# A matrix product with seven-product blocks: a third row pair multiplied directly before the summed pairs begin

## The chip, the cores and the metric

The kernel runs on one core of a Trainium2 chip. The metric is the device time of one execution in microseconds (us). A profile of one execution per run gives a span, from the first to the last recorded instruction, which is shorter than the time. TensorE multiplies, VectorE and ScalarE empty its accumulators (PSUM) and convert types, GpSimd converts and adds, SyncE issues most transfers. The trace also holds the clock that TensorE was granted, as a share of full speed; 0.50 is called cold. A record is one entry of the trace, with a start and a length.

## The reference

```
x: 16 x 512 x 768 fp32        w_qkv: 768 x 2304 fp32
qkv = matmul(x, w_qkv)
return stack([qkv[..., :768], qkv[..., 768:1536], qkv[..., 1536:]])
```

It is one product of an 8192 x 768 matrix with a 768 x 2304 matrix, cut into three parts.

## The kernel before

Rows are taken in 32 pairs of 128-row blocks. The 2304 columns are two quads of 1024 and a remainder of 256. A quad of a pair takes seven block products of three matmuls, 21 in place of 24, if sums of rows and of weights are formed first. These sums are not there at the start, so the first two pairs are multiplied directly in bf16, one weight block of 512 columns after the other, while the rest of the weights comes in. Pair 2 is the first summed one: TensorE turns its fp32 rows so that GpSimd can sum them.

```
def block(q, c, w, groups, cast_next):        # direct, for pairs 0 and 1
    ps = [bank() for _ in range(4)]
    for js, tiles in groups:
        for n in tiles:                       # 4 row blocks
            ... matmul(ps[n], xb[p][:, j, rows], w[:, j, :]) for j in js
            ... cast_next(p); copy ps[n] to the output tile; store
...
busy(11)                                      # warming matmuls on zeros
cast_rows(0); turn_bf16(0)
busy(4)
cast_rows(1); ...; turn_bf16(1)
...
cast(0, 1, 1, bt0, nc.gpsimd)                 # second half of the next block
nc.gpsimd.tensor_copy(out=b22[0][:], in_=stage[0, 1, 1])
block(0, 0, b1[0], singles, lambda h: None)   # 24 matmuls
rem(0)                                        # 12 matmuls of 256 columns
rem(1)
turn_fp32(2)                                  # TensorE turns fp32 rows
cast(0, 0, 1, bt0, act)                       # first half of the next block
round_x(2)
sums_x(2)
...
block(0, 1, bt0, halves, cast_next(1, 0, b1[1]))
block(1, 0, b1[1], halves, cast_next(1, 1, bt1))
block(1, 1, bt1, halves, lambda h: None)
...
for p in range(2, NP): two(quad(p, 0), quad(p, 1), early)   # summed pairs
```

## Time and profile before

| | before |
|---|---|
| time, median of 3 (lowest to highest) | 368.38 us (368.31 to 368.80) |
| the profiled execution: time, span | 369.94, 368.2 us |
| TensorE busy | 98% of the span |
| first summed product starts at | 37.73 us |
| one summed pair | 9.54 + 1.33 = 10.87 us |

The page gives busy shares; the chain that ended last gives, from the first to the last instruction, what held up the end, in pieces of start, length and work. Where the chain is on TensorE without a break, only fewer or faster matmuls help.

### The profile page before, as it was taken

How to read it: one execution, taken by the hardware profiler on the slowest of the kernel's cores; microseconds unless marked ns; L12 is line 12 of the kernel's file. 1: busy time of each engine (PE TensorE's matmuls, PEld its weight loads, DVE VectorE, ACT ScalarE, POOL GpSimd, SP SyncE). 2: the span in 40 equal slices, each digit the busy share in tenths (PEclk: the TensorE clock that was granted, in tenths of full speed). 3: DMA queues.
4: the chain of work that ended last, by engine and by line, in shares of the span. 5: the costliest groups of instructions: out<-in, count | busy, mean ns of one | idle time of the engine just before them, and what ended most of it. 6: DMA issues, size and time to landing. Idle time of an engine off the chain costs nothing.

```text
span 368.2 us, 5286 instructions
## 1 busy us (share of the span) xinstructions
PE 359.8 (98%) x1791; PEld 246.9 (67%) x1791; DVE 229.7 (62%) x235; ACT 185.5 (50%) x307; POOL 191.9 (52%) x191
## 2 busy tenths in 40 slices
PE   7979999999999999999999999999999999999995
PEld 3634666677767677766667776766776666777673
DVE  3399766555666655576655566665557665556632
ACT  4557645454444454544545444445454454544442
POOL 1089935466544456644456654445664444665420
PEclk9989999999999999999999999999999999999998
DMA  7999898889988899998888998888899889899767
GB/s 295 381 385 339 268 281 278 291 280 301 317 283 276 271 302 280 309 310 273 280 292 280 301 316 285 276 278 297 276 313 306 276 261 309 271 309 319 267 232 280
DMA packets 80618, 108.09 MB, mean 294 GB/s; under 512 B 4816, under 2 KB 60368, under 8 KB 80592
## 3 DMA queue, kind: packets, MB, share of 16 engines
q1 hardware_dynamic: 64640, 95.96, 79.8%
q10 hardware_dynamic: 15952, 11.80, 10.1%
q8 instruction: 14, 0.23, 0.3%
q14 instruction: 12, 0.10, 0.1%
HBM read 32.24 MB, written 75.50 MB: 293 GB/s over the span
## 4 chain that ended last, share of the span: by engine, by line
PE 96%; DMA 1%; ACT 1%; DVE 0%; issue 0%
PE ps L212 78%; PE ps L262 12%; PE ps L386 6%; DMA xin<-in_x_dram 1%; PE ps L169 0%; PE ps L158 0%; ACT bt L374 0%; ACT xc L140 0%; ACT xb L140 0%; ACT xf L140 0%; ACT orem L317 0%; DVE xb L139 0%
## 5 line engine op out<-in xcount | busy, mean ns | idle before, releaser
L212 PE MATMUL ps<-t,s 128*128 128x512 f32 x720 | 194.5, 412 | 0.0
L212 PEld LDWEIGHTS ps<-t,s 128*128 128x128 f32 x720 | 133.2, 188 | 32.0
L175 POOL CAST xb<-xf 128x1536 bf16<-128x1536 f32 x30 | 45.5, 1515 | 139.3 <-DVE xf L124 139.3
L212 PE MATMUL ps<-b,xb 128*128 128x512 bf16 x360 | 88.1, 381 | 0.0
L124 DVE STREAM_TRANSPOSE xf<-xin 128x1536 f32<-128x1536 f32 x29 | 86.9, 2996 | 0.9 <-DMA xin<-in_x_dram 0.8
L246 DVE TENSOR_TENSOR o<-o,ps 128x512 f32<-128x512 f32 x60 | 41.3, 688 | 62.4 <-PE ps L212 62.3
L240 DVE TENSOR_TENSOR o<-o,ps 128x512 f32<-128x512 f32 x60 | 41.3, 688 | 57.3 <-ACT o L239 57.3
L212 PEld LDWEIGHTS <-xb 128*128 128x128 bf16 x360 | 30.5, 98 | 44.5 <-issue 15.7
L239 ACT ACTIVATE o<-ps 128x512 f32<-128x512 f32 x60 | 36.0, 600 | 46.8 <-PE ps L212 46.8
L226 ACT ACTIVATE o<-ps 128x512 f32<-128x512 f32 x60 | 35.9, 599 | 45.2 <-DVE o L246 40.6
L233 ACT ACTIVATE o<-ps 128x512 f32<-128x512 f32 x60 | 36.0, 600 | 43.4 <-PE ps L212 43.4
L262 PE MATMUL ps<-w_rem,xb 128*128 128x256 bf16 x384 | 47.5, 273 | 0.0
L212 PE MATMUL ps<-b,s 128*128 128x512 f32 x180 | 46.5, 393 | 0.0
L262 PEld LDWEIGHTS <-xb 128*128 128x128 bf16 x384 | 35.0, 98 | 12.4 <-issue 8.4
L212 PEld LDWEIGHTS ps<-b,s 128*128 128x128 f32 x180 | 33.8, 188 | 8.0
L230 DVE TENSOR_TENSOR o<-o,ps 128x512 f32<-128x512 f32 x60 | 37.6, 669 | 2.0 <-ACT o L226 1.3
L243 ACT ACTIVATE o<-ps 128x512 f32<-128x512 f32 x60 | 35.9, 598 | 4.8 <-ACT orem L317 0.4
L184 POOL TENSOR_TENSOR s<-s,xf 128x384 fp32r<-128x384 f32 x30 | 31.9, 1064 | 2.4
L187 POOL TENSOR_TENSOR s<-xf,s 128x384 fp32r<-128x384 f32 x30 | 32.1, 1069 | 0.0
L183 POOL TENSOR_TENSOR s<-xf 128x384 fp32r<-128x384 f32 x30 | 31.9, 1064 | 0.0
L185 POOL TENSOR_TENSOR s<-xf 128x384 fp32r<-128x384 f32 x30 | 31.6, 1054 | 0.0
L272 ACT ACTIVATE orem<-ps 128x512 f32<-128x512 f32 x31 | 18.6, 599 | 22.7 <-PE ps L262 22.7
(40 smaller groups left out, 122.7 us busy)
## 6 DMA issues: line engine op xcount, KB each, us to landing
out_dram<-o SPq DMA_DIRECT2D x62, 768.0 KB, 4.9
out_dram<-o SPq DMA_DIRECT2D x65, 256.0 KB, 4.6
xin<-in_x_dram SPq DMA_DIRECT2D x60, 192.0 KB, 6.7
xin<-in_x_dram ACTq DMA_DIRECT2D x56, 192.0 KB, 5.7
out_dram<-orem SPq DMA_DIRECT2D x31, 256.0 KB, 2.3
st<-in_w_qkv_dram SPq DMA_DIRECT2D x6, 768.0 KB, 14.1
xin<-in_x_dram SPq DMA_DIRECT2D x3, 768.0 KB, 5.8
st<-in_w_qkv_dram SPq DMA_DIRECT2D x6, 256.0 KB, 6.2
```

Source lines behind the costliest of these rows:

```text
L124: nc.vector.transpose(t[:].rearrange("p j (g b) -> p g j b", b=G), xin.pop(p)[:].rearrange("p g (a j) -> p g j a", a=G),)
L175: nc.gpsimd.tensor_copy(out=xb[p][:], in_=xf[p][:])
L187: g.tensor_tensor(s[:, 4], a12, s[:, 2], op=sub)
L212: nc.tensor.matmul(ps[:], lhs[j], rhs[j], start=(start and j == 0), stop=(j == KH - 1), skip_group_check=True,)
L226: nc.scalar.activation(c11, u.x[:], ident)
L230: nc.vector.tensor_tensor(c11, c11, u.z[:], op=add)
L233: nc.scalar.activation(c12, u.x[:], ident)
L239: nc.scalar.activation(c22, u.x[:], ident)
L240: nc.vector.tensor_tensor(c22, c22, u.y[:], op=add)
L243: nc.scalar.activation(c21, u.x[:], ident)
L246: nc.vector.tensor_tensor(c12, c12, u.y[:], op=add)
L262: nc.tensor.matmul(ps, xb[p][:, j, r * P:(r + 1) * P], w_rem[:, j, :], start=(j == 0), stop=(j == KT - 1), skip_group_check=True,)
```

## The change

It makes three pairs direct instead of two. Pair 2's rows are cast to bf16 by VectorE and turned in bf16, and twelve matmuls of pair 2 on the first weight block stand where TensorE waited for the second block. VectorE casts the second block. Each direct block has six row blocks for four, so the next weights are wanted later. Pair 3 becomes the first summed one.

```
-    cast(0, 1, 1, bt0, nc.gpsimd)
-    nc.gpsimd.tensor_copy(out=b22[0][:], in_=stage[0, 1, 1])
-    block(0, 0, b1[0], singles, lambda h: None)
+    block(0, 0, b1[0], singles, nothing)
     rem(0)
     rem(1)
-    turn_fp32(2)
-    cast(0, 0, 1, bt0, act)
-    round_x(2)
-    sums_x(2)
+    cast_rows(2, False)                      # VectorE alone
+    turn_rows(2, False)                      # bf16, copied out by VectorE alone
+    block(0, 0, b1[0], halves((4, 5)), nothing)
+    for h in range(2):
+        cast(0, h, 1, bt0, dve)
     for n in range(1, 5):
         sum_w(0, n)
-    nc.gpsimd.tensor_copy(out=b22[1][:], in_=stage[1, 1, 1])
-    block(0, 1, bt0, halves, cast_next(1, 0, b1[1]))
+    dve.tensor_copy(out=b22[0][:], in_=stage[0, 1, 1])
+    block(0, 1, bt0, halves(range(6)), cast_next(1, 0, b1[1]))
     ... the other two blocks likewise, then rem(2)
-    for p in range(2, NP):
+    for p in range(3, NP):
```

The fp32 identity matrix and `turn_fp32` go away; the loads of pairs 3 and 4 are issued earlier.

More of the change, by code (lines that the diff above doesn't have):

```diff
@@ L135, in load_rows, with copy_halves, cast_rows @@
         nc.sync.dma_start(xin[p][:], rows.rearrange("(r m) k -> m r k", m=P))
-    def copy_two(dst, src):
+    def copy_halves(dst, src, two):
         nc.vector.tensor_copy(out=dst[0], in_=src[0])
-        nc.scalar.activation(dst[1], src[1], ident)
+        if two:
+            nc.scalar.activation(dst[1], src[1], ident)
+        else:
+            nc.vector.tensor_copy(out=dst[1], in_=src[1])
     xc = {}
-    def cast_rows(p):
+    def cast_rows(p, two=True):
         src = xin.pop(p)
@@ L148, in cast_rows, with turn_rows @@
             halves = (slice(0, K // 2), slice(K // 2, K))
-            copy_two([xc[p][:, r, n] for n in halves], [src[:, r, n] for n in halves])
-    def turn_bf16(p):
+            copy_halves([xc[p][:, r, n] for n in halves], [src[:, r, n] for n in halves], two)
+    def turn_rows(p, two=True):
         c = xc.pop(p)
@@ L157, in turn_bf16 @@
             for j in range(KT):
-                nc.tensor.transpose(ps[:, j, :], cols[:, j, :], eye_b[:])
+                nc.tensor.transpose(ps[:, j, :], cols[:, j, :], eye[:])
             ks = (slice(0, KH), slice(KH, KT))
-            copy_two([xb[p][:, n, r * P:(r + 1) * P] for n in ks], [ps[:, n, :] for n in ks])
-    def turn_fp32(p):
-        src = xin.pop(p)
-        xf[p] = xf_pool.tile([P, KT, 2 * P], fp32, name="xf")
-        for r in range(2):
-            cols = src[:, r, :].rearrange("m (p j) -> m j p", j=KT)
-            ps = [ps_pool.tile([P, KH, P], fp32, name="ps") for _ in range(2)]
-            for j in range(KT):
-                nc.tensor.transpose(ps[j // KH][:, j % KH, :], cols[:, j, :], eye[:])
-            ks = (slice(0, KH), slice(KH, KT))
-            copy_two([xf[p][:, n, r * P:(r + 1) * P] for n in ks], [t[:] for t in ps])
+            copy_halves(
+                [xb[p][:, n, r * P:(r + 1) * P] for n in ks], [ps[:, n, :] for n in ks], two
+            )
     def round_x(p):
@@ L341, in last @@
         rem_stored(1)
+    NS = 3
     zero = w_pool.tile([P, CB], bf16, name="zero")
@@ L348 @@
     nc.scalar.activation(tiny[:], zero[:, :1], ident)
-    eye = w_pool.tile([P, P], fp32, name="eye")
+    eye = w_pool.tile([P, P], bf16, name="eye")
     make_identity(nc, eye)
-    eye_b = w_pool.tile([P, P], bf16, name="eye_b")
-    make_identity(nc, eye_b)
     load_rows(1)
@@ L358 @@
     load_blocks(0, 1)
-    o0 = [quad(p, 0) for p in range(2)]
     load_blocks(1, 0)
     load_blocks(1, 1)
-    o1 = [quad(p, 1) for p in range(2)]
+    load_x(3, nc.sync)
+    quads = [[quad(p, q) for p in range(NS)] for q in range(2)]
     def busy(n):
@@ L378, in block @@
     def block(q, c, w, groups, cast_next):
-        ps = [bank() for _ in range(4)]
+        ps = {}
         for js, tiles in groups:
@@ L384, in block @@
                 p, r = divmod(n, 2)
+                if n not in ps:
+                    ps[n] = bank()
                 for j in js:
@@ L393, in block, with halves @@
                     cast_next(p)
-                o = (o0, o1)[q][p]
-                nc.scalar.activation(o.o[:, r, c * CB:(c + 1) * CB], ps[n][:], ident)
+                u = quads[q][p]
+                nc.scalar.activation(u.o[:, r, c * CB:(c + 1) * CB], ps[n][:], ident)
                 if c == 1 and r == 1:
-                    store_quad(o)
-    halves = [(range(h * KH, (h + 1) * KH), range(4)) for h in range(2)]
+                    store_quad(u)
+    def halves(tiles):
+        return [(range(h * KH, (h + 1) * KH), tiles) for h in range(2)]
     singles = [((0, ), (0, 1)), ((1, ), (0, 1)), ((0, 1), (2, 3))]
@@ L407, in cast_k, with cast_next @@
         dve.tensor_copy(out=b1[0][:, j, :], in_=stage[0, j // KH, 0][:, j % KH, :])
+    def cast_next(q, c, w):
+        return lambda p: p < 2 and cast(q, p, c, w, act)
+    def cast_k(j):
+        dve.tensor_copy(out=b1[0][:, j, :], in_=stage[0, j // KH, 0][:, j % KH, :])
+    nothing = lambda p: None
     busy(11)
     cast_rows(0)
-    turn_bf16(0)
+    turn_rows(0)
     busy(4)
@@ L415 @@
     cast_k(1)
-    turn_bf16(1)
+    turn_rows(1)
     for j in range(2, KT):
@@ L422 @@
     bt1 = bt_pool.tile([P, KT, CB], bf16, name="bt")
-    def cast_next(q, c, w):
-        return lambda h: cast(q, h, c, w, act)
-    cast(0, 1, 1, bt0, nc.gpsimd)
-    nc.gpsimd.tensor_copy(out=b22[0][:], in_=stage[0, 1, 1])
-    block(0, 0, b1[0], singles, lambda h: None)
+    block(0, 0, b1[0], singles, nothing)
     rem(0)
     rem(1)
-    turn_fp32(2)
-    cast(0, 0, 1, bt0, act)
-    round_x(2)
-    sums_x(2)
+    cast_rows(2, False)
[3 more added lines that the diff above has]
+        cast(0, h, 1, bt0, dve)
     for n in range(1, 5):
         sum_w(0, n)
-    nc.gpsimd.tensor_copy(out=b22[1][:], in_=stage[1, 1, 1])
-    block(0, 1, bt0, halves, cast_next(1, 0, b1[1]))
-    load_x(3, nc.sync)
-    block(1, 0, b1[1], halves, cast_next(1, 1, bt1))
-    block(1, 1, bt1, halves, lambda h: None)
+    dve.tensor_copy(out=b22[0][:], in_=stage[0, 1, 1])
+    block(0, 1, bt0, halves(range(6)), cast_next(1, 0, b1[1]))
+    load_x(4, nc.sync)
+    block(1, 0, b1[1], halves(range(6)), cast_next(1, 1, bt1))
+    block(1, 1, bt1, halves(range(6)), nothing)
+    rem(2)
     t_1 = [tq_pool.tile([P, 2, KH, CB], f32r, name=f"t_1{n}", tag="tq") for n in range(2)]
     ts[1] = [t_1[n // 2][:, n % 2] for n in range(4)]
-    for n in range(1, 5):
-        sum_w(1, n)
-    for p in range(2, NP):
+    sum_w(1, 1)
+    sum_w(1, 2)
+    transpose(3)
+    round_x(3)
+    sums_x(3)
+    sum_w(1, 3)
+    sum_w(1, 4)
+    dve.tensor_copy(out=b22[1][:], in_=stage[1, 1, 1])
+    for p in range(NS, NP):
         def early():
```

## The prediction

> **What bounds the kernel now.** I read the page first (busy shares and the line of granted clock), then the chain that ended last piece by piece, then busy time by windows over the stretch that the change rewrites, then the groups of instructions there.
>
> ```profile
> PE 359.8 (98%) x1791; PEld 246.9 (67%) x1791; DVE 229.7 (62%) x235; ACT 185.5 (50%) x307; POOL 191.9 (52%) x191
> ...
> PE 96%; DMA 1%; ACT 1%; DVE 0%; issue 0%
> ```
>
> TensorE is the bound, nearly without a hole, so the change counts by what it does to TensorE's own stream. The chain shows where that stream is not full:
>
> ```profile
> 8.95 5.18 PE ps L386 x24
> 14.12 2.66 PE ps L262 x24
> 16.79 1.63 PE ps L169 x12
> 18.41 0.02 issue
> 18.43 0.49 ACT xf L140
> 18.93 1.38 ACT bt L374
> 20.31 0.04 issue
> 20.35 17.39 PE ps L386 x72
> 37.73 7.45 PE ps L212 x33
> 45.19 1.33 PE ps L262 x12
> 46.52 9.54 PE ps L212 x42
> ```
>
> Columns are start, length in us, what. The first direct block takes 5.18 us for 24 matmuls of 512 columns (0.2158 us each). The fp32 turning of pair 2 (L169) then takes 1.63 us. From 18.42 to 20.35 the chain leaves TensorE: it waits on ScalarE, which copies the last turned quarter and casts the first half of the next weight block (L374). After that 72 matmuls take 17.39 us, where 72 x 0.2158 = 15.54. The windows say why:
>
> ```profile
> 18.42:20.35 1.93, 0.00 (x1) 0.00 (x0) 1.90 (x3) 1.86 (x2) 0.93 (x1) 1.00 1.05 386
> 20.35:21.35 1.00, 1.00 (x5) 0.49 (x5) 1.00 (x1) 0.00 (x0) 1.00 (x1) 0.91 1.05 385
> 21.35:22.35 1.00, 1.00 (x4) 0.35 (x3) 1.00 (x1) 0.00 (x0) 1.00 (x2) 0.50 1.05 387
> 22.35:23.35 1.00, 1.00 (x3) 0.30 (x2) 1.00 (x2) 0.49 (x1) 1.00 (x1) 0.50 1.06 391
> 23.35:24.35 1.00, 1.00 (x4) 0.42 (x3) 1.00 (x1) 0.99 (x1) 1.00 (x1) 0.50 1.06 391
> 24.35:25.35 1.00, 1.00 (x6) 0.40 (x5) 1.00 (x1) 0.00 (x0) 1.00 (x2) 0.89 1.05 385
> ```
>
> After the length come PE, PEld, DVE, ACT and POOL busy, then the granted clock, DMA share and GB/s. The clock falls to 0.50 about a microsecond after the hole and stays there some 3.5 us: 17.39 - 15.54 = 1.85 us lost. Hole and cold clock together are 1.93 + 1.85 = 3.78 us, and the DMA share near 1.05 with 386 GB/s says that this is also the stretch where loads are the other limit. From 37.73 on, every summed pair is the same: 42 matmuls in 9.54 us and 12 remainder matmuls in 1.33, so 10.87 us, thirty times to the end.
>
> **What the Trainium skill says.** (1) "TensorE: Matmul & The Clock Gate", Part 1: the clock is gated to half when a free-running window of about 3.4 us was idle, and comes back after as long a busy one. The trace agrees: 0.50 for about 3.5 us, after the hole of 1.93. (2) The same page, Part 4, says that transposes do not count as busy for that gate. That would fit here: 1.63 us of turning plus the 1.93 us hole are 3.56 us without a plain matmul, about one window; the trace alone cannot show it. (3) The same page, Back-to-back issue gap: 512/2.4 + 2.5, about 216 ns, for 512 columns; the block's 215.8 ns agrees. Summed pairs take 9.54/42 = 227 ns, so summed matmuls are somewhat dearer. (4) "SBUF — State Buffer", Who interferes with whom: VectorE with two SBUF inputs and GpSimd's reads lock each other out, one blocking the other for a whole instruction. The trace agrees: L107 took 1.75 us while GpSimd still stood and 2.6 us in the mean of its in-place form while GpSimd worked.
>
> **The change part by part.** All on TensorE's stream, from 16.79 (end of the two remainders), where nothing before differs except one identity matrix less on GpSimd.
>
> *Turning pair 2.* Twelve fp32 transposes (1.63) become twelve bf16 ones; the chain has such twelve, for pair 1, in 0.95. Saves 0.68. Its inputs: the queue issued the rows of pair 2 at 7.03 and they landed 8.3 us later, at 15.3. VectorE, free since 13.94, casts four pieces of 128x384 in about 0.31 us each (two for pair 0 took 0.63 in the timeline): first row block at 16.0, second at 16.65, before 16.79. So no wait there. TensorE turns until 17.74. VectorE copies the first piece out after six transposes, near 17.7, and the next three at about 0.36 each to 18.8; tile 4 can start at about 17.75, tile 5 near 18.45. I allow 0.1 us of small gaps.
>
> *Twelve matmuls of pair 2 on the first block.* 12 x 0.2158 = 2.59, so to about 20.4. This is new work, and it stands exactly in the old hole.
>
> *Weight block bt.* VectorE, not ScalarE and GpSimd, casts both halves. From L407 (512 elements, 0.426) and L420 (768, 0.559) I extrapolate 0.97 us for 1536. First half 18.8 to 19.8, wanted at 20.4; second half landed at 19.42 (GpSimd's wait for it ended there), cast by 20.75, wanted 18 matmuls later at 24.3. No hole, so no cold clock: 1.93 + 1.85 saved.
>
> *Three blocks of six tiles* are 108 x 0.2158 = 23.31 us, to 43.7, then the remainder of pair 2, 1.33, to 45.05.
>
> *One summed pair less.* -10.87.
>
> The sum: direct pair 48 x 0.2158 + 1.33 = 11.69 against 10.87 summed, +0.82; turning -0.68; hole -1.93; cold clock -1.85; small gaps +0.1. Total -3.54 us. The same by positions: the first summed pair starts at 45.05 instead of 37.73 with 29 pairs to run instead of 30: 45.05 - 37.73 - 10.87 = -3.55.
>
> *What lies beside.* ScalarE gives up one cast but has 24 evictions (0.60) for 16, and the four casts of the second half's weights (1.48). In block (0,1) it works from 22.9 (landing of the third weight block) to about 30.2; its next cast is done by 31.7 and wanted at 36. VectorE does sums, at 1.75 each without GpSimd beside them, to about 32, transposes pair 3 (3.0), then contends with GpSimd's rounding and sums (GpSimd's took 2.0 to 3.0 each in such a stretch) until some 42.5. Rounded rows of pair 3 are there at 38 to 40, wanted at 45; the sum for the first summed product by 44, wanted at 47.
>
> **The rivals.**
> (a) *The hole moves.* Six banks of eight are held by each block, and one engine now does casts and copies that two did. If VectorE is late by over 0.6 us with bt, or the rows of pair 2 land late, TensorE waits again, and 2 us of turning and waiting together might bring the cold clock back. For: the DMA is full and the times are close (16.65 against 16.79, 19.8 against 20.4). Against: there are 2.6 us of matmuls between the turning and the next block, so no window is empty. It would make 365.5 to 367.
> (b) *Transfers become the bound.* All loads but the last now include pair 3 at once, then three pairs' stores in 18 us. By my count the weights end at 28.9 (last issue 14.4, 14.5 to landing); pair 3 (0.79 MB), two remainders (0.52), three quads (3.15) and pair 4 (0.79) are 5.25 MB, and at 380 GB/s land by 42.7. The transpose of pair 4 wants it at 46. If strided rows run at 300 GB/s, it is 46.4, with several us before TensorE would wait for it. Output buffers: the sixth quad takes the first quad's buffer, free near 35.5, wanted at 36 to 37. Against this rival: slack in each place. For: five buffers now hold six quads. At worst +1 to +3 us, 366 to 368.
> (c) *The direct pair just costs more*, with the hole hidden elsewhere: +0.82 - 0.68, nearly the same as before, 368.5. It would need a wait as long as the old one; nothing in the order shows one.
> (d) *More than counted.* A gain over 2% needs 7.4 us; all that TensorE loses between 9 and 46 us is 3.8. I see no source for it.
>
> **Range and chances.** 368.38 - 3.54 = 364.8. Low end 363.8 if the gaps vanish and runs scatter (0.3% of each other); high end 366.5 for part of (a) or (b). That is 1% faster, inside the 2% either way: same 0.96, faster 0.02, slower 0.02.
>
> **What would show it right or wrong.** Right: no hole over 0.3 us in TensorE's stream between 9 and 46 us; granted clock 1.00 in every window there; twelve turns in about 0.95 us; direct matmuls at 0.216 us throughout; first summed product at about 45.0; pairs of 10.87 us after; VectorE's first sums near 1.75 us. Wrong: a clock of 0.50 in any window from 17 to 46; TensorE waiting for VectorE's xb or bt; summed pairs longer than 10.9 us; TensorE waiting for pair 3's or 4's rows or sums.

## The result

The changed kernel took 367.26 us (median of 4, 366.91 to 367.66) against 368.35 (median of 4, 368.16 to 368.80). The ratio is 0.9969, with a 95% interval of 0.9952 to 0.9986. Ratios are the mean time of one kernel's fast runs over that of the other's of the same rounds, so they are not quite the ratio of the medians quoted. So 1.1 us was won, not 3.5, and the time lies above the range.

And yet the profile of the changed kernel is nearly the one that was foretold. Its page, with busy shares and the engines of the chain:

```profile
PE 358.0 (98%) x1797; PEld 243.8 (67%) x1797; DVE 225.8 (62%) x239; ACT 182.4 (50%) x304; POOL 173.7 (48%) x180
...
PE 97%; DMA 1%; ACT 1%; DVE 0%; issue 0%
```

Its chain that ended last, by time (start, length, what):

```profile
8.92 5.18 PE ps L381 x24
14.10 2.65 PE ps L256 x24
16.75 0.35 PE ps L161 x6
17.10 0.02 issue
17.12 0.37 DVE xb L139
17.49 0.05 issue
17.54 26.07 PE ps L381 x120
43.61 1.31 PE ps L256 x12
44.92 7.45 PE ps L206 x33
52.37 1.33 PE ps L256 x12
```

The wait of 1.93 us is gone: between the turning's last record and the next matmul TensorE stands for 0.12 us (17.42 to 17.54), since the second half of the turning runs during VectorE's first copy. The turning with its first copy takes 0.79 us, then 120 direct matmuls stand in one piece of 26.07 us (0.2173 each), and the first summed product starts at 44.92 us, where 45.05 was predicted. The windows (length; PE, PEld, DVE, ACT, POOL busy; granted clock, DMA share, GB/s) show no cold clock:

```profile
20.35:21.35 1.00, 1.00 (x6) 0.49 (x5) 0.51 (x1) 0.58 (x1) 0.00 (x0) 1.00 1.04 383
21.35:22.35 1.00, 1.00 (x7) 0.44 (x5) 1.00 (x2) 0.00 (x0) 0.00 (x0) 1.00 1.06 389
```

The span fell from 368.2 to 364.8 us. But this execution took 366.91 us, 2.13 more than its span; the execution profiled before took 369.94, 1.79 more than its span of 368.155. So there were two questions: why do other executions of the kernel before take 1.6 us less than the profiled one, and where does the changed kernel lose time that its TensorE stream does not show?

### The profile page after: what moved, and what is told of

It reads as the page before. It is cut to its first block, busy times and chain, and to the rows that moved or that the text cites. A ratio compares the mean times of both kernels' runs of the same rounds, so it can differ in the third digit from the quotient of the medians.

```text
span 364.8 us, 5274 instructions
## 1 busy us (share of the span) xinstructions
PE 358.0 (98%) x1797; PEld 243.8 (67%) x1797; DVE 225.8 (62%) x239; ACT 182.4 (50%) x304; POOL 173.7 (48%) x180
## 4 chain that ended last, share of the span: by engine, by line
PE 97%; DMA 1%; ACT 1%; DVE 0%; issue 0%
PE ps L206 76%; PE ps L256 12%; PE ps L381 9%; DMA xin<-in_x_dram 1%; PE ps L161 1%; ACT xc L141 0%; ACT xb L141 0%; DVE xb L139 0%; ACT orem L311 0%
## 5 line engine op out<-in xcount | busy, mean ns | idle before, releaser
L206 PE MATMUL ps<-t,s 128*128 128x512 f32 x696 | 188.0, 412 | 0.0
L206 PEld LDWEIGHTS ps<-t,s 128*128 128x128 f32 x696 | 128.7, 188 | 30.9
L169 POOL CAST xb<-xf 128x1536 bf16<-128x1536 f32 x29 | 43.9, 1514 | 171.6 <-DVE xf L124 160.1
L206 PE MATMUL ps<-b,xb 128*128 128x512 bf16 x348 | 85.2, 381 | 0.0
L240 DVE TENSOR_TENSOR o<-o,ps 128x512 f32<-128x512 f32 x58 | 39.9, 688 | 59.3 <-PE ps L206 59.2
L234 DVE TENSOR_TENSOR o<-o,ps 128x512 f32<-128x512 f32 x58 | 39.8, 687 | 54.1 <-ACT o L233 54.1
L233 ACT ACTIVATE o<-ps 128x512 f32<-128x512 f32 x58 | 34.8, 600 | 45.2 <-PE ps L206 45.2
L220 ACT ACTIVATE o<-ps 128x512 f32<-128x512 f32 x58 | 34.7, 599 | 43.3 <-DVE o L240 34.6
L227 ACT ACTIVATE o<-ps 128x512 f32<-128x512 f32 x58 | 34.8, 600 | 41.9 <-PE ps L206 41.9
L206 PE MATMUL ps<-b,s 128*128 128x512 f32 x174 | 44.9, 393 | 0.0
L224 DVE TENSOR_TENSOR o<-o,ps 128x512 f32<-128x512 f32 x58 | 36.5, 669 | 2.3 <-ACT o L220 1.3
L237 ACT ACTIVATE o<-ps 128x512 f32<-128x512 f32 x58 | 34.7, 598 | 4.5 <-ACT orem L311 0.4
L178 POOL TENSOR_TENSOR s<-s,xf 128x384 fp32r<-128x384 f32 x29 | 30.1, 1038 | 2.3
L177 POOL TENSOR_TENSOR s<-xf 128x384 fp32r<-128x384 f32 x29 | 30.9, 1066 | 0.0
L181 POOL TENSOR_TENSOR s<-xf,s 128x384 fp32r<-128x384 f32 x29 | 29.5, 1019 | 0.0
L179 POOL TENSOR_TENSOR s<-xf 128x384 fp32r<-128x384 f32 x29 | 29.2, 1006 | 0.0
```

The lines of the kernel that those rows point to most:

```text
L169: nc.gpsimd.tensor_copy(out=xb[p][:], in_=xf[p][:])
L206: nc.tensor.matmul(ps[:], lhs[j], rhs[j], start=(start and j == 0), stop=(j == KH - 1), skip_group_check=True,)
L220: nc.scalar.activation(c11, u.x[:], ident)
L224: nc.vector.tensor_tensor(c11, c11, u.z[:], op=add)
L227: nc.scalar.activation(c12, u.x[:], ident)
L233: nc.scalar.activation(c22, u.x[:], ident)
```

## The experiments

Thirteen runs were made, e1 to e13; e1, e2 and e11 are unchanged kernels. All gave correct results. The times quoted are those of each run's rounds beside the kernel before on the same chip.

### The two kernels again, and the hole filled

The two kernels were run unchanged for their spread (e1, e2). The third run (e3) puts nine spare matmuls into the hole:

```
     turn_fp32(2)
+    busy(9)
     cast(0, 0, 1, bt0, act)
```

Expected of the kernel before, again:

> The kernel before, unchanged, to see its spread. Theory A (the clock fell to half in the profiled execution of before only by the phase of a free-running window; in most executions the hole passes without it): spans in two groups, most near 368.2 - 1.85 = 366.3 us with a granted clock of 0.997 to 1.0, some near 368.2 with 0.992; median time 368.4. Rival B (the cold clock is there in every execution and the changed kernel loses its gain elsewhere): all spans 368.0 to 368.5, all clocks 0.992.

Of the changed kernel, again:

> The changed kernel, unchanged, to see its spread. The four runs so far lie at 366.9 to 367.0 and at 367.5 to 367.7. Theory A: the same two groups 0.6 us apart, no clock below 0.997, median 367.2; against the kernel before 0.997. Rival B: a slower group with a lower clock, 1.5 us or more apart.

Of the filled one:

> The kernel before with nine spare matmuls on zeros (9 x 0.216 = 1.94 us) right after the fp32 turning of pair 2, as long as the hole, so that TensorE idles no more there and waits no longer than before. Theory A: only the executions with the cold clock gain, so the median falls by 0 to 0.5 us (367.9 to 368.4), all spans near 366.3, no window at clock 0.50 between 17 and 30 us. Rival B: every execution gains the 1.85 us of cold clock, median 366.5, ratio 0.995.

Measured: the kernel before 368.41 us (368.19 to 368.85), and its profile has a span of 366.6 us. The changed kernel 367.36 (366.87 to 367.61). The filled one 368.48 (368.19 to 368.95), ratio 0.9989 with an interval of 0.9968 to 1.0011: nothing won. The eleven runs of the kernel before on the same chip were eight at 368.19 to 368.64 and three at 369.87, 369.89 and 370.50. In the chain of the kernel before, again, the hole is there as in the first profile:

```profile
16.89 1.62 PE ps L169 x12
18.52 0.02 issue
18.54 0.49 ACT xf L140
19.03 1.38 ACT bt L374
20.41 0.04 issue
20.45 0.38 PE ps L386
...
36.16 7.45 PE ps L212 x33
```

The hole lasts from 18.52 to 20.45, again 1.93 us. But the direct blocks after it end at 36.16, so they take 15.71 us, not 17.39, and the windows there show the full clock:

```profile
21.35:22.35 1.00, 1.00 (x6) 0.46 (x5) 1.00 (x1) 0.00 (x0) 1.00 (x2) 1.00 1.05 389
22.35:23.35 1.00, 1.00 (x6) 0.48 (x5) 1.00 (x2) 0.43 (x1) 1.00 (x1) 1.00 1.04 383
```

So the cold clock itself costs 17.39 - 15.71 = 1.68 us; the prediction's 1.85 had set the cold blocks against 0.2158 us per matmul, where the usual execution takes 0.218. Theory A holds: the profile on which the prediction rested had caught one of the rarer, longer executions. Filling the hole does not help the usual execution, since there the hole costs its own length only, and matmuls on zeros fill that length to no end.

### Another look at the kernel before: a rule for the cold clock

The trace also records when TensorE's clock changes. If the clock follows free-running windows of 3.413 us, as the Trainium skill has it ("TensorE: Matmul & The Clock Gate", Part 1), the end of a window can be read at the first rise of the clock, W, and all later ends are W plus multiples of 3.413 us.

> One more look at the kernel before, for the phase rule. The clock record gives the moment W of the first rise; windows end at W plus multiples of 3.413 us. Theory A: where one of these ends falls between 20.4 and 21.8 (so that the hole from 18.4 to 20.4 lies within one window), that is W between 3.3 and 4.8, the clock falls to 0.50 at that end for 3.41 us, and the time is 369.8 or more; for any other W it stays at 1.00 and the time is below 369. Rival: clock and W are unrelated.

It took 369.84 us (a single run, so its state is unknown): a cold execution, with W at 4.37, as theory A said. All traces of kernels that still have the hole, from their clock records:

```
run                        W      hole            end of window    clock after it   time
first profile of before    4.09   18.42 to 20.35  21.16            0.50 from 21.16  369.94
e11, before                4.37   18.28 to 20.21  21.43            0.50 from 21.43  369.84
e1, before                 5.89   18.52 to 20.45  19.54 and 22.95  1.00             368.37
e13, before, one load more 6.62   18.84 to 20.78  20.27 and 23.69  1.00             368.62
e5, before, 117 memsets    6.03   18.61 to 20.56  19.68 and 23.09  1.00             370.64 (below)
```

The two cold falls come at W + 5 x 3.413 to the hundredth. The trace of e11 has 0.50 for just one window:

```profile
21.43:24.84 3.41, 3.41 (x10) 1.21 (x8) 3.41 (x2) 1.48 (x1) 3.41 (x3) 0.50 1.05 386
24.84:26.00 1.16, 1.16 (x7) 0.49 (x6) 1.16 (x2) 0.61 (x2) 1.16 (x1) 1.00 1.06 390
```

In these five traces, where the hole lies within one window the next one is cold; where a window's end cuts it, the clock stays at 1.00. The filled kernel (W at 4.00) and the changed one (W at 4.22) had the phase of the cold executions and stayed at 1.00, since the hole was closed. Of 50 timed runs of the kernel before (4 beside the first result, 6 of its own again, 40 beside the other experiments) eight took 369.8 us or more. Of 56 timed runs of kernels with the hole closed (the changed kernel and all others but e1, e5, e11 and e13) none lay over 0.8 us above its own fastest. (Of the other kernels with a hole, e5 has two of six and e13 one of four at 1.2 us or more above their fastest, with the lower mean clock.) So the cold clock cost 1.68 us in about one execution in six, some 0.3 us on average, and nothing in a median.

### The end of the program

In the changed kernel the end of the program is longer than in any profiled execution of the kernel before: its last matmul ends 4.5 us before the span's end, for 4.2 in the three traces of the kernel before. The last records of the engines are drains and semaphores, in which they wait for each other; they are called the closing barrier here. SyncE's own waits over the last 4.2 us, for the kernel before (second profile) and the changed one (us in total, times, longest):

```profile
SPq L487 <- PEq L487: 0.6, 2, 0.4
```

```profile
SPq L492 <- PEq L492: 0.9, 2, 0.7
```

The release is put down to TensorE's queue as the last to arrive at a barrier. The single records of that closing barrier, in us before the end of the span, show who was late (e8 and e5 are told of below):

```
                          before (e1)   changed   e8       e5
GpSimd drain              -0.261        -0.572    -0.261   -0.558
GpSimd semaphore, next    -0.183        -0.191    -0.183   -0.191
```

Between the two lie 0.08 us before and 0.38 in the changed kernel. Of blocks of instructions (8192 bytes each, on queue 14, which the page labels "instruction") the end of the trace has one before the change and two after it. All of them start after the last record (at 1.13 us before the change, at 0.49 and 1.62 after it), so none that is seen is what the barrier waited for. GpSimd's program had become eleven records shorter; so the theory was that the end of one block of its program now falls into the barrier. The test (e4) is to make it as long as before again, by memsets on one spare column at the start, and, as a mirror (e5), to bring the kernel before to the same length within a block, on the assumption that a block holds 128 instructions (198 + 128 = 326 records):

```
     make_identity(nc, eye)
+    pad = w_pool.tile([P, 1], fp32, name="pad")
+    for _ in range(11):                      # 117 in the mirror
+        nc.gpsimd.memset(pad[:], 0.0)
```

> The changed kernel with eleven one-column GpSimd memsets on a spare tile at the start, while GpSimd idles, so that GpSimd's program is as long as before the change (209 records, not 198). Theory T (in the closing barrier GpSimd waits 0.31 us for a block of its own instructions, because its program got eleven instructions shorter and the end of a block fell into the barrier; the same costs another 0.34 us after the last record): the time from GpSimd's drain to its next semaphore falls from 0.38 to 0.08 us, time less span from 2.11 to 1.77, median 366.7 instead of 367.3. Rival U (the longer end belongs to the stores or to something else of the change): no difference, 367.3.

> The mirror image: the kernel before with 117 such memsets, which makes GpSimd's program as long as the changed one's plus 128 instructions[...], one block of 8192 bytes. GpSimd idles until 19.4 us, and they take about 0.04 to 0.1 us each from 1.8 on, so nothing waits for them. Theory T: the closing barrier grows by 0.31 us and the time less span by 0.34, median 369.05 instead of 368.4. Rival U: 368.4.

Both came out slower than either theory said: 368.01 us (367.89 to 368.35) for the first and 370.67 (370.51 to 371.86) for the mirror. The barrier did what theory T says, as the table shows for the mirror: it got long where it had been short. In the first its two records lie at -0.261 and -0.182, short again. T's other half failed: the time less the span stayed at 2.15 in the first, where T had 1.77, and at 1.84 in the mirror, where T had 0.34 more. And something else came in: in both, 42 summed matmuls took 9.59 us, not 9.54, 29 or 30 times over (and in the mirror the memsets, which lasted until 22.17, put off GpSimd's cast of the second block, and TensorE waited another 0.32 us). A run with one warming matmul fewer on top of the first (e7) has the same flaw:

```
-    busy(11)
+    busy(10)
```

> As the changed kernel with eleven memsets, and ten instead of eleven warming matmuls at the start. In the executions in which the clock rises late (at 7.1 us in the second profile of the changed kernel, at 4.2 in the first), eleven cold ones end at 6.06 and hold up the first turning by 0.43 us, ten end at about 5.6, when the rows are there. Expected: early-rise executions as with eleven memsets alone (366.2 to 366.3), late-rise ones 0.3 to 0.4 us shorter, median 366.4. Rival: fewer warming matmuls make the clock rise later and give the gain back, median 366.7 or more.

It took 368.08 us (367.87 to 368.24). The 366.4 expected is out of reach for that reason; beside the first, which has the same flaw, nothing is won.

Two runs took this apart. (A pool is a stretch of the on-chip memory, SBUF, from which tiles are taken.) In one (e8) the spare column lies in a pool opened last, so that no other tile moves; in the other (e9) it lies where it did, with a single memset:

```
+    pad_pool = ctx.enter_context(tc.tile_pool(name="pad", bufs=1))   # after all others
...
+    pad = pad_pool.tile([P, 1], fp32, name="pad")
```

> The eleven memsets again, on a spare tile in a pool opened last, so that no other tile moves. Theory L (the spare column moved later tiles by a few bytes, and that alone made 42 summed matmuls take 9.59 instead of 9.54 us): pairs of 9.54 again, closing barrier short (0.08 us from drain to semaphore), so the 0.31 us of the barrier show in the whole: fastest runs 366.6, median 366.9 to 367.0. Rival M (GpSimd's longer program or the memsets slow TensorE): 9.59 again and a median of 368.0.

> The spare column where it was at first, in the middle of the weights' pool, and one memset only. Theory L: pairs of 9.59, long barrier as in the changed kernel less at most a little, median 368.2 to 368.6. Rival M: pairs of 9.54, median 367.3.

Theory L holds. With the column last, the kernel took 366.69 us (366.60 to 367.08, ratio 0.9948); with the column in the middle and hardly a memset, 368.57. One summed pair in the chain, first of the run with the column last, then of the other:

```profile
108.11 2.08 PE ps L207 x9
110.20 0.07 issue
110.27 7.39 PE ps L207 x32
```

```profile
108.40 2.10 PE ps L206 x9
110.50 0.07 issue
110.57 7.43 PE ps L206 x32
```

From the end of one remainder to the start of the next are 9.55 and 9.60 us. (A matmul is missing from these records; the time is not.) The spacing of the remainders, pair after pair, is 10.87 us in every trace with no column or with the column last, and 10.92 in e4, e5, e7 and e9. So a spare column of 4 bytes per partition costs 0.05 us in every summed pair by its place alone; which tile's new place does it, and why, was not separated. And with that out of the way, the eleven memsets are worth what the barrier lost: the span is 364.5 for 364.8, and the fastest run 366.60 for 366.87. In e9, with one record more than the changed kernel, the late place in GpSimd's barrier begins one record earlier: 0.34 us stand before the drain, where the others have 0.04, and the barrier is longer by another 0.14. That too fits a place counted in records of the program.

The warming was tried once more on the good version (e10):

> Eleven memsets on the tile in the last pool, and ten warming matmuls instead of eleven: a version that could beat all. Ten cold matmuls end at 5.5 to 5.6 instead of 6.06. Expected: fastest runs 366.5, slowest 367.0 instead of 367.5, median 366.7. Rival: the clock rises later for it and nothing is won beside the run before it (366.9 to 367.0).

It took 366.74 us (366.55 to 367.09). The 366.7 expected was met, but e8 has 366.69 with eleven, so nothing is won; why is not shown. What it was aimed at is real, though. Two groups some 0.6 us apart show in the changed kernel's runs, and its second profile, in which the clock rose only at 7.08, shows where they come from:

```profile
1.19 4.88 PE ps L361 x11
6.06 1.23 PE ps L161 x12
```

Eleven cold warming matmuls lasted until 6.06, when the first rows had been ready for some 0.4 us, and the turning itself ran at half clock; the direct blocks started at 9.62, not at 8.92 as in the first profile (rise at 4.22).

### Outside of the span

There remained 0.34 us (the second half of theory T): the time less the span was 2.13 to 2.15 in seven runs of the changed kernel and its forms, 1.79 to 1.84 in forms of the kernel before, 1.91 in the one of the next section. Two runs were added for it (e12, e13). The first, on top of e8, also brings the programs of ScalarE and VectorE to their former lengths:

```
+    for _ in range(7):
+        nc.scalar.activation(pad2[:], zero[:, :1], ident)
+    nc.vector.memset(pad3[:], 0.0)
```

The second is the kernel before with one load made two, which gives SyncE 385 records in place of 384, as in the changed kernel.

> As the changed kernel with eleven memsets on the last pool's tile, and besides seven one-column ScalarE copies and one VectorE memset on spare columns at the start, so that ScalarE (530 records) and VectorE (446) too have programs as long as before the change. Open point: every form of the changed kernel shows a time 2.13 to 2.15 us over its span, forms of the kernel before 1.74 to 1.91. Theory S (the end of ScalarE's or VectorE's program fell into an unlucky place, as GpSimd's did): time less span near 1.8, fastest run 366.3. Rival (SyncE, which has 385 records for 384, or something else): 2.14, fastest run 366.6.

> The kernel before with the load of the remainder's weights as two loads of half the size, so that SyncE's program has one or two records more (385 or 386 for 384). If SyncE's length makes the difference outside the span: time less span near 2.14 in place of 1.74 to 1.82, the fastest run near 368.5. If not: near 1.8, fastest run 368.2.

The first took 366.27 us (366.20 to 366.36, ratio 0.9930), 1.79 over its span. The second took 368.64 (368.05 to 369.90), also 1.79 over its span. So it is the length of ScalarE's or VectorE's program, not of SyncE's; which of the two was not separated. In the traces the last block of instructions on queue 14 starts 1.62 to 1.66 us after the last record in the seven runs at 2.13 to 2.15, and 1.09 to 1.29 in all others, e12 among them; whose block it is they do not show. The first of these runs is the fastest kernel.

### Is the third pair needed to close the hole?

Run e6 keeps two direct pairs and closes the hole by another order:

```
-    cast(0, 1, 1, bt0, nc.gpsimd)
     ...
     rem(0)
-    rem(1)
     turn_fp32(2)
-    cast(0, 0, 1, bt0, act)
+    rem(1)
+    cast(0, 0, 1, bt0, dve)
+    cast(0, 1, 1, bt0, act)
```

> The kernel before with its two summed-from-the-start pairs kept as they are and the hole closed another way: the second remainder comes after the turning of pair 2, VectorE casts the first half of the next weight block and ScalarE the second. No third direct pair. If the gain of the change is the closing of the hole (1.93 us) and not the third pair itself (which costs 0.8): hole at most 0.3 us, the first summed product at 34.5 instead of 36.1, no execution with a cold clock, median 366.7 to 367.0. If the third pair matters in itself: no better than 368.0.

It took 367.28 us (367.21 to 367.35, ratio 0.9963), as fast as the changed kernel, but not the 366.7 to 367.0 expected. The hole at 18.4 is gone and the first summed product starts at 35.01, only 1.15 us earlier than in the kernel before, since a new wait opens. Its chain:

```profile
9.07 13.86 DMA st<-in_w_qkv_dram
22.93 0.02 issue
22.95 1.49 ACT b L374
24.45 0.04 issue
24.49 10.52 PE ps L386 x48
```

The first half of the third weight block lands at 22.93, is cast until 24.45, and TensorE, which had finished the second block, waits 0.69 us for it. That is what the third pair is for: it makes each direct block half as long again, so that the third weight block is wanted at 28.0 and not at 23.8; its first half is ready at 24.4 there too. In the changed kernel no such wait exists. The third pair has its price, 0.80 us, and keeps TensorE out of the loads' way. So the hole can be closed without it. Put on the same count of pairs, the changed kernel's stream is still 0.96 us ahead of e6 (44.92 - 10.87 = 34.05 against 35.01), and its longer ends take 0.53 of that back (0.31 in the barrier, and 2.13 against 1.91 after it).

## Why the prediction was wrong

**The step that failed** is "No hole, so no cold clock: 1.93 + 1.85 saved", as far as the 1.85 goes. The loss is real, 1.68 us when measured against the usual execution, and the change does remove it, but it belongs to about one execution in six. The runs put 0.3 us on average in its place, and none in the usual execution. The warning stood in the data: the profiled execution took 369.94 us, the three timed ones 368.31 to 368.80.

**What the sum left out** is the end of the program: 0.31 us in the closing barrier and 0.34 us after the last record, both from the lengths of programs (e8 and e12 take them away). "What lies beside" looked at engines' work only.

The rest of the steps, between the changed kernel's first profile and the second one of before, where neither has a cold clock:

| step | predicted | measured |
|---|---|---|
| turning pair 2, with gaps | -0.58 | 1.63 to 0.79: -0.84 |
| hole | -1.93 | -1.93 |
| third pair direct | +0.82 | (26.07 + 1.31) - (15.71 + 10.87) = +0.80 |
| cold clock | -1.85 | 0 |
| ends of the programs | none | +0.31 + 0.34 = +0.65 |
| sum | -3.54 | -1.32 |

The two executions of the table, 366.91 and 368.37 us, differ by 1.46; 0.14 of that lies before the rewritten stretch (it starts at 16.75 and 16.89), and 1.32 is left, as the sum says. The fastest runs of e2 and e1 differ by 1.32 too. The medians differ by 1.1, and they also carry which runs had a late rise of the clock at the start. In a cold phase (W at 4.09 and 4.22) the two kernels took 369.94 and 366.91 us, which is -3.03, and without the 0.65 at the ends it would be -3.68, for -3.54 predicted: there the sum was nearly right, with the turning 0.26 better than said and the cold clock 0.17 smaller.

**The rivals.** (a) and (b), a moved hole and the loads as the bound, did not come about; but in e6, without the third pair, TensorE does wait for a load and its cast, 0.69 us. (c) was wrong, as the pair's price is what was said and the hole is closed. (d), a gain over 2%, did not come either. Of the signs named, the first summed product came at 44.92 (about 45.0 expected), direct matmuls at 0.217 (0.216), pairs at 10.87 or 10.88 (10.87), the first sum of weights on VectorE in 1.75 us, no gap over 0.12 us after the turning and no cold window; these were right. The twelve turns took 0.67 us (16.75 to 17.42), not about 0.95. None of the signs could show that the comparison was with an unusual execution.

**Two readings that did not hold.** Point (2), that turning is as good as idling for the clock, is contradicted by e13 (last section). In point (4), GpSimd did not stand through the whole first sum in the profile before: the sum ran from 18.51 to 20.25 and GpSimd began a cast at 19.42. The changed kernel shows the point more plainly: all six sums of weights that end before GpSimd starts at 35.93 take 1.75 or 1.76 us, and the one that begins while GpSimd works takes 3.02.

## What to carry to other kernels

Before a loss in a profile is put on the account of a change, compare that execution's own time with the timed ones: a loss that is not in the median is not won in the median. Where TensorE waits for data, look for work that is needed anyway and that also puts off the next demand on the loads: spare matmuls in the hole won nothing here (e3), the third pair did. And beside a gain of 0.3%, the 1.1 us here, the place of a tile (0.05 us in each of some 30 pairs) and the lengths of engines' programs (0.65 us) count as much as a rearrangement, so a spare tile belongs in a pool of its own and an experiment that adds instructions needs a control.

## What the Trainium skill lacked or had wrong

- "TensorE: Matmul & The Clock Gate", Part 1, gives one idle window as the condition for the half clock. Here a hole of 1.93 us within a window of 3.413 was enough (the rest of that window held 0.67 us of turning and 0.81 us of matmuls in the first profile). The page's window length is right: falls came at W + 5 x 3.413 to the hundredth. That one gap in mid-kernel splits a kernel's runs in two groups, 8 of 50 some 1.6 us longer, is not said there.
- The same page, Part 4, says that transposes do not count as busy for the clock in the same way. In e13 a window from 16.86 to 20.27 held 0.36 us of matmuls, 1.62 of fp32 turning and 1.43 of idling, and the clock stayed at 1.00; were turning idle, that is 3.05 us, more than the 2.60 us of the window that brought the clock down in the first profile. So fp32 turning counted as work here.
- No page says that the place of a small tile changes the rate of matmuls: 9.54 to 9.59 us for 42 of them from a spare column of 4 bytes per partition. "SBUF — State Buffer", Operand start alignment, speaks of what is legal and says itself that it timed nothing.
- No page says that the length of an engine's program moves the end of an execution: 0.38 us in place of 0.08 in the closing barrier for GpSimd, and another 0.34 us after the last record from the length of ScalarE's or VectorE's program. Of the pages, "Runtime: NRT & Kernel Launch" is where it would belong. That a fetch is what is waited for is not shown, as the blocks seen at the end start after the last record; shown is only that the lengths decide.
